# All elementwise work with two tensor inputs goes to the vector engine, and the tasks no longer name an engine

## The chip, the cores and the metric

The kernel runs on one core of one Trainium2 chip. The metric is the time of one execution on the device in microseconds, as the median of several runs. The core's engines are named as the profile names them: PE is TensorE (matrix products and transposes), PEld its weight loads, DVE is VectorE, ACT is ScalarE, POOL is GpSimd, SP is SyncE, which issues the loads.

## What is computed

A network of two layers over 256 latent tokens and 256 context tokens, model width 1024. Each layer has a half-step feed-forward part, a token mixer, and a second half-step feed-forward part. Each of these three is normed on the way in and on the way out, and its shift, scale and gate come from a conditioning vector:

```python
def half_ffn(x, mod, k, norm_g, w):
    h = modulated_norm(x, mod, k, norm_g)          # rms_norm * (1 + scale) + shift
    return gated_residual(x, swiglu(h, *w), mod, k, norm_g, FFN_RESIDUAL)   # x + weight*gate*rms_norm(y)
...
y, y_c = token_mixers(h, hc, not last, ...)        # windowed attention, dense attention, mLSTM; merged; @ w_out
x = gated_residual(x, y, mod, 1, norm_g[l], 1.0)
x = half_ffn(x, mod, 2, norm_g[l], ffn2)
if not last:
    ctx = gated_residual(ctx, y_c, mod_c, 1, norm_g[l], 1.0)
    ctx = half_ffn(ctx, mod_c, 2, norm_g[l], ffn2)
```

The hidden width of the feed-forward part is 2816. All data are float32, and the output is the latent stream, 256 x 1024.

## The kernel before

A float32 product is made of three products of two shorter parts. Each operand is split into a high part (a copy into the type fp32r, by ScalarE) and a low part (the value less its high part); `mm3` (L192) multiplies high by high, high by low and low by high (L194 to L196). Weights come in units of 128 partitions by up to 1024 columns, 512 KB. `cvt_unit` (L155) converts one: `hi` on ScalarE (L162), `lo` by a two-input subtraction (L163) on the engine that the task names. `run_tasks` (L167) walks through a list of tasks, each a triple of weight units, a function and a list of engines; it converts units two tasks ahead of their use and issues their loads on SP's queue three units further ahead. There are four buffers for raw units and five each for `hi` and `lo`; a raw buffer comes free when its `lo` is done, and the next load into it waits for that.

The parts in order of time, in microseconds of the profiled execution: feed-forward part of layer 0 (to about 400), its mixer (to 1000), its second feed-forward part (to 1345), the first of layer 1 (to 1738), its mixer (to 2110), and the last, for the latent tokens only.

The end of each part is a chain of norms. `closing` (L503) finishes the output half by half. `post_half` (L552) takes square sums on ScalarE (L560) and multiplies each half by its gate (L563); `post_finish` (L566) computes the inverse root of the mean square and updates the residual (L574); `prenorm_stat` (L437) takes the square sums of the new rows (L444), an inverse root again, and writes the normalised rows `t` (L449 on VectorE, L451 on ScalarE), which TensorE transposes (L466) for the next part. The inverse root is `rsqrt` (L205): a seed and three Newton steps on columns of 1, 2, 8 or 16 numbers, each instruction waiting for the one before (L211 to L220). A part is done for the latent and then the context tokens, so each change of part has two such chains.

In the mixer, `q_rows` (L751) rotates the rows of the normed queries (`rope`, L743 to L749) or scales them (`times_g`, L774); `k_rows` (L790 on) norms and rotates the keys; `k_cols` (L813) splits their transposes (L826 to L828). `logsig` (L1104 to L1126) computes the forget gates of the mLSTM. The attention scores are written at L1012, and L1043 scales some of the probabilities on GpSimd, with one tensor input and a column of factors.

Tables name the engines: `BOTH_E`, `ONE_E`, `EARLY_E` and `GP` put some of the feed-forward units' subtractions on GpSimd, and the wrapper `pool(...)` in `mixer_tasks` those of most of the query, value and convolution units. The rest go to VectorE. The order of the instructions on each engine is not written out: a scheduler chooses it when the kernel is built, from the tasks' order, a priority (`urgent`) and its own estimates of durations. Each engine then runs its list in order.

## Time and profile before

| | |
|---|---|
| median of 3 runs | 2339.59 us (2339.14 to 2345.08) |
| span of the profiled execution, its own time | 2339.1 us |
| TensorE busy | 2243.5 us, 96% |
| VectorE busy | 1574.0 us, 67%, 2709 instructions |
| ScalarE busy | 1025.0 us, 44% |
| GpSimd busy | 198.7 us, 8%, 115 instructions |
| chain that ended last | TensorE 83%, VectorE 11%, ScalarE 4%, GpSimd 0% |
| mean granted clock of TensorE | 0.98 |

The chain is followed back from the last instruction, at each step to what released it. The granted clock is a share of TensorE's full speed; the two levels that occur are 1 (2.4 GHz) and 0.5 (1.2 GHz). A wait is put down to the engine whose work came last.

### The profile page before, as it was taken

The page shows a single profiled execution, that of the slowest core. Times are in us where ns is not written, and L with a number is a line of the kernel's source. Part 1 is how long each engine was busy: PE and PEld are TensorE (multiplying, and loading weights), DVE is VectorE, ACT ScalarE, POOL GpSimd, SP SyncE. Part 2 cuts the span into 40 slices and gives each one's busy share as a digit, 9 for nine tenths or more (in the row PEclk, how much of TensorE's full clock was granted, in tenths as well). Part 3 has the DMA queues.
Part 4 walks back from the last instruction along what each step waited for, and adds up shares of the span by engine and source line. Part 5 has one row for each costly group of instructions (what it writes and reads, how often), then busy time and mean ns, then how long its engine had stood idle before and what let it go on. Part 6 is the DMA issues. An engine that isn't in the chain of part 4 may idle for free.

```text
span 2339.1 us, 30561 instructions
## 1 busy us (share of the span) xinstructions
PE 2243.5 (96%) x11666; PEld 1848.6 (79%) x11666; DVE 1574.0 (67%) x2709; ACT 1025.0 (44%) x1637; POOL 198.7 (8%) x115
## 2 busy tenths in 40 slices
PE   7999999899999999999999989999999899996998
PEld 4877777776678888888878788787878668996997
DVE  3987775788776654664444378778768677867555
ACT  3322222567887433442222253222235488754443
POOL 0000001123410000200000020000012220003001
PEclk9999999999999999999999999999999899998999
DMA  7756563411122224434343327656643103464664
GB/s 274 224 191 184 164 215 103 133 63 38 37 89 75 81 84 135 138 122 135 117 126 117 113 90 221 193 186 192 194 126 118 55 28 118 154 227 143 189 186 144
DMA packets 123523, 322.98 MB, mean 138 GB/s; under 512 B 12392, under 2 KB 25768, under 8 KB 122608
## 3 DMA queue, kind: packets, MB, share of 16 engines
q1 hardware_dynamic: 110224, 309.83, 41.8%
q10 hardware_dynamic: 13152, 11.21, 1.6%
q8 instruction: 91, 1.49, 0.3%
q14 instruction: 56, 0.46, 0.1%
HBM read 316.72 MB, written 4.28 MB: 137 GB/s over the span
## 4 chain that ended last, share of the span: by engine, by line
PE 83%; DVE 11%; ACT 4%; issue 1%; DMA 1%; POOL 0%; ACTq 0%; DVEq 0%
PE ps L194 25%; PE ps L195 25%; PE ps L196 25%; PE ps L1244 1%; PE ps L1015 1%; DVE sm L220 1%; PE ps L1055 1%; DVE lo L163 1%; PE ps L1012 1%; DVE sm L219 1%; PE ps L364 1%; PE ps L1213 1%; DVE slot L574 1%; PE ps L1070 1%; PE ps L466 1%
## 5 line engine op out<-in xcount | busy, mean ns | idle before, releaser
L162 ACT ACTIVATE hi<-raw 128x1024 fp32r<-128x1024 f32 (+1 forms) x444 | 456.0, 1031 | 769.7 <-PE ps L195 261.8
L194 PE MATMUL ps<-slot,hi 128*128 128x512 f32 (+1 forms) x2232 | 777.6, 350 | 7.1 <-ACT slot L189 4.9
L195 PE MATMUL ps<-slot,hi 128*128 128x512 f32 (+1 forms) x2232 | 775.8, 348 | 0.5 <-DVE slot L190 0.4
L196 PE MATMUL ps<-slot,lo 128*128 128x512 f32 (+1 forms) x2232 | 773.3, 347 | 0.0
L163 DVE TENSOR_TENSOR lo<-raw,hi 128x1024 fp32r<-128x1024 f32 (+2 forms) x395 | 475.1, 1205 | 287.6 <-ACT hi L162 285.6
L194 PEld LDWEIGHTS ps<-slot,hi 128*128 128x128 f32 x2232 | 419.6, 189 | 75.6 <-ACT slot L189 7.1
L196 PEld LDWEIGHTS ps<-slot,lo 128*128 128x128 f32 x2232 | 421.1, 189 | 57.5
L195 PEld LDWEIGHTS ps<-slot,hi 128*128 128x128 f32 x2232 | 421.0, 189 | 56.1 <-DVE slot L190 1.4
L194 PE MATMUL ps<-hi,slot 128*128 128x512 f32 (+2 forms) x1048 | 404.4, 386 | 3.0 <-DVE slot L828 1.9
L195 PE MATMUL ps<-lo,slot 128*128 128x512 f32 (+2 forms) x1048 | 402.0, 384 | 4.0 <-DVE lo L163 2.5
L196 PE MATMUL ps<-hi,slot 128*128 128x512 f32 (+2 forms) x1048 | 401.4, 384 | 2.9 <-DVE slot L190 2.9
L356 DVE SCALAR_TENSOR_TENSOR t<-raw,sc,t 128x1024 f32<-128x1024 f32 x224 | 280.4, 1281 | 130.8 <-DMA raw<-in_w_ada_dram 130.6
L194 PEld LDWEIGHTS ps<-hi,slot 128*128 128x128 f32 x1048 | 199.0, 190 | 49.1 <-issue 8.9
L196 PEld LDWEIGHTS ps<-hi,slot 128*128 128x128 f32 x1048 | 198.8, 190 | 44.3 <-DVE slot L190 3.1
L195 PEld LDWEIGHTS ps<-lo,slot 128*128 128x128 f32 x1048 | 199.0, 190 | 43.8 <-DVE lo L163 4.9
L163 POOL TENSOR_TENSOR lo<-raw,hi 128x1024 fp32r<-128x1024 f32 (+1 forms) x49 | 116.8, 2389 | 683.4 <-ACT hi L162 508.8
L189 ACT ACTIVATE slot<-t 128x512 fp32r<-128x512 f32 (+1 forms) x138 | 80.3, 594 | 183.4 <-DVE t L606 158.1
L563 POOL TENSOR_TENSOR slot<-slot,slot 128x512 f32<-128x512 f32 x20 | 30.3, 1524 | 1321.4 <-DMA raw<-in_w_down_dram 733.3
L606 DVE TENSOR_TENSOR t<-ps,t 128x512 f32<-128x512 f32 (+1 forms) x88 | 54.7, 622 | 87.9 <-PE ps L196 86.7
L190 DVE TENSOR_TENSOR slot<-t,slot 128x512 fp32r<-128x512 f32 (+1 forms) x138 | 88.6, 651 | 6.9 <-ACT slot L189 6.5
L1017 DVE TENSOR_REDUCE sm<-ps 128x1 f32<-128x512 f32 (+1 forms) x96 | 55.9, 593 | 13.1 <-PE ps L1015 12.6
L466 PE MATMUL ps<-ident,t 128*128 128x128 f32 x176 | 30.5, 331 | 34.4 <-DVE t L449 33.4
(194 smaller groups left out, 1911.3 us busy)
## 6 DMA issues: line engine op xcount, KB each, us to landing
raw<-in_w_gu_dram SPq DMA_DIRECT2D x176, 512.0 KB
raw<-in_w_ada_dram SPq DMA_DIRECT2D x128, 512.0 KB
raw<-in_w_down_dram SPq DMA_DIRECT2D x92, 512.0 KB
raw<-in_w_fm_dram SPq DMA_DIRECT2D x64, 512.0 KB
raw<-in_w_br_dram SPq DMA_DIRECT2D x24, 512.0 KB
raw<-in_w_out_dram SPq DMA_DIRECT2D x24, 512.0 KB
slot<-in_w_ada_dram SPq DMA_DIRECT2D x16, 512.0 KB
raw<-in_w_down_dram SPq DMA_DIRECT2D x20, 256.0 KB
```

Of the source, the lines that this page charges most:

```text
L162: self.nc.scalar.activation(out=hi, in_=raw, func=AF.Copy)
L163: eng.tensor_tensor(out=lo, in0=raw, in1=hi.bitcast(F32), op=ALU.subtract)
L189: self.nc.scalar.activation(out=hi, in_=src, func=AF.Copy)
L190: self.nc.vector.tensor_tensor(out=lo, in0=src, in1=hi.bitcast(F32), op=ALU.subtract)
L194: mm(out, lh, rh, start=start, stop=False, **kw)
L195: mm(out, lh, rl, start=False, stop=False, **kw)
L196: mm(out, ll, rh, start=False, stop=stop, **kw)
L356: v.scalar_tensor_tensor(out=acc, in0=units[0], scalar=c, in1=acc, op0=ALU.mult, op1=ALU.add)
L466: nc.tensor.transpose(pt[:, o:o + P], xn[b][:, c * P:(c + 1) * P], self.ident)
L563: eng.tensor_tensor(out=self.y_half(st, tb, n), in0=src[q], in1=self.Gt[tb // 2][:, n * 512:(n + 1) * 512], op=ALU.mult)
L606: nc.vector.tensor_tensor(out=hid[:, :W], in0=ps[:, :W], in1=hid[:, :W], op=ALU.mult)
L1017: v.tensor_reduce(out=mx[:, :1], in_=ps[:, :nkey], axis=AX.X, op=ALU.max)
```

## The change

Every weight subtraction is issued on VectorE, and so are all the products with the gate (L563), the rotation and the scaling of the query rows. The tables of engines and the wrapper are gone, and a task's optional third entry is now the look-ahead. L1043 stays on GpSimd. Comments are removed, so lines move up by four to ten.

```diff
-    def cvt_unit(self, st, eng):
+    def cvt_unit(self, st):
...
-        eng.tensor_tensor(out=lo, in0=raw, in1=hi.bitcast(F32), op=ALU.subtract)
+        self.nc.vector.tensor_tensor(out=lo, in0=raw, in1=hi.bitcast(F32), op=ALU.subtract)
...
-            want = min(len(keys), use + (rest[1] if len(rest) > 1 else LA_CVT))
+            want = min(len(keys), use + (rest[0] if rest else LA_CVT))
...
-        out = [one(ga, i) for i in range(nu)] + [(keys[1], both, BOTH_E(v, g))]
+        out = [one(ga, i) for i in range(nu)] + [(keys[1], both)]
...
-        return out + [(*one(gb, i), [ONE_E(v, g)[i]], *la(i)) for i in range(nu)]
+        return out + [(*one(gb, i), *la(i)) for i in range(nu)]
...
-            eng = nc.vector if ds or (last and q == 0) else nc.gpsimd
-            eng.tensor_tensor(out=self.y_half(st, tb, n), in0=src[q], in1=self.Gt[tb // 2][:, n * 512:(n + 1) * 512],
-                              op=ALU.mult)
+            nc.vector.tensor_tensor(out=self.y_half(st, tb, n), in0=src[q], in1=self.Gt[tb // 2][:, n * 512:(n + 1) * 512],
+                                    op=ALU.mult)
...
-                eng = nc.gpsimd if part == 0 and q < GP else nc.vector
-                out.append(([("gu", l, i, f0 + q // 2, q % 2)], gu(q // 2, q % 2), [eng]))
+                out.append(([("gu", l, i, f0 + q // 2, q % 2)], gu(q // 2, q % 2)))
...
-            self.rope(u, q, 8, tb, self.cosg[0], self.sing[0], nc.gpsimd, q)
+            self.rope(u, q, 8, tb, self.cosg[0], self.sing[0], q)
         else:
-            self.times_g(q, q, 8, 0, nc.gpsimd)
+            self.times_g(q, q, 8, 0)
...
-        side = gates[:1] + pool(qb[:1]) + gates[1:2] + pool(qb[1:] + vm_[nv:va]) + gates[2:] + pool(vm_[va:vb]) + qcols(1) + pool(vm_[vb:])
+        side = gates[:1] + qb[:1] + gates[1:2] + qb[1:] + vm_[nv:va] + gates[2:] + vm_[va:vb] + qcols(1) + vm_[vb:]
         na = 4 * len(qtb)
-        out += weave(att[:na], side) + weave(att[na:], pool(conv))
+        out += weave(att[:na], side) + weave(att[na:], conv)
```

The scheduler's order shifts with it. Three places show how.

VectorE between the second layer's mixer and the last feed-forward part, in the second half of the first tokens' norm chain. Before (`sm` are the inverse root's columns, L563 the gate product, `lo` a weight's low part):

```order
L574 SCALAR_TENSOR_TENSOR slot_17592<-slot_17646,sm_17703,slot_17592 128x1024
L163 TENSOR_TENSOR lo_17760<-raw_17666,hi_17759 128x1024
L211 TENSOR_SCALAR sm_17717<-sm_17714 128x1
L212 TENSOR_SCALAR sm_17718<-sm_17717 128x1
L216 SCALAR_TENSOR_TENSOR sm_17719<-sm_17718,sm_17717 128x1
L220 SCALAR_TENSOR_TENSOR sm_17718<-sm_17719,sm_17718 128x1
L563 TENSOR_TENSOR slot_17646<-ps_17730,slot_17590 128x512
L216 SCALAR_TENSOR_TENSOR sm_17719<-sm_17718,sm_17717 128x1
```

After the change VectorE has, from the same residual update on:

```order
L567 SCALAR_TENSOR_TENSOR slot_17592<-slot_17646,sm_17703,slot_17592 128x1024
L159 TENSOR_TENSOR lo_17773<-raw_17668,hi_17772 128x1024
L159 TENSOR_TENSOR lo_17791<-raw_17670,hi_17790 128x1024
L206 TENSOR_SCALAR sm_17717<-sm_17714 128x1
L556 TENSOR_TENSOR slot_17646<-ps_17730,slot_17590 128x512
L207 TENSOR_SCALAR sm_17718<-sm_17717 128x1
L159 TENSOR_TENSOR lo_17880<-raw_17763,hi_17879 128x1024
L211 SCALAR_TENSOR_TENSOR sm_17719<-sm_17718,sm_17717 128x1
L159 TENSOR_TENSOR lo_17884<-raw_17776,hi_17883 128x1024
L215 SCALAR_TENSOR_TENSOR sm_17718<-sm_17719,sm_17718 128x1
L556 TENSOR_TENSOR slot_17646<-ps_17765,slot_17590 128x512
```

Subtractions that stood in GpSimd's list now stand between the steps of the inverse root.

VectorE at the split of the keys in the second layer's mixer. Before, `s` are the forget gates' numbers, the copy and subtraction at L827 and L828 split the keys:

```order
L1115 TENSOR_TENSOR s_2530_14631<-s_2529_14630 128x32
L1116 TENSOR_SCALAR s_2531_14632<-s_2530_14631 128x32
L1118 SCALAR_TENSOR_TENSOR s_2531_14632<-s_2531_14632,s_2530_14631 128x32 x7
L1119 SCALAR_TENSOR_TENSOR s_2531_14632<-s_2531_14632,s_2529_14630 128x32
L1120 TENSOR_SCALAR s_2531_14632<-s_2531_14632 128x32
L1121 SCALAR_TENSOR_TENSOR s_2531_14632<-s_2527_14627,s_2531_14632 128x32
L1126 COPY s_2532_14650<-s_2531_14632 128x4x4 x2
L827 COPY slot_14529<-slot_14529 64x512
L828 TENSOR_TENSOR slot_14529<-ps_14530,slot_14529 64x512
```

After the change, from the gate add (L1097) at the same place on, VectorE has:

```order
L1097 TENSOR_TENSOR s_2527_14627<-gm_14463,gateb_13948 128x64
L1100 SCALAR_TENSOR_TENSOR s_2528_14629<-s_2527_14627 128x32
L1115 COPY s_2532_14650<-s_2527_14627 128x4x4 x2
L159 TENSOR_TENSOR lo_15131<-raw_14499,hi_15130 128x1024
L818 COPY slot_14529<-slot_14529 64x512
L819 TENSOR_TENSOR slot_14529<-ps_14530,slot_14529 64x512
L818 COPY slot_14541<-slot_14541 64x512
L819 TENSOR_TENSOR slot_14541<-ps_14542,slot_14541 64x512
L778 TENSOR_TENSOR slot_14553<-ps_14555,slot_14553 64x4x128
```

The split stood behind the whole computation of the forget gates; now it stands ahead of it, behind one more weight subtraction.

TensorE between the first feed-forward part and the mixer of layer 0; `ps_3074` and `ps_3081` are outputs of the feed-forward part, `ps_3116` on receives the transposes of the normalised rows. Before:

```order
L194 MATMUL ps_3081<-hi_2912,slot_2252 128x512
L195 MATMUL ps_3081<-lo_2913,slot_2252 128x512
L196 MATMUL ps_3081<-hi_2912,slot_2254 128x512
L466 MATMUL ps_3116<-ident,t_480_3011 128x128
L466 MATMUL ps_3116<-ident,t_481_3013 128x128
```

After the change, at the same place, TensorE has, once the products with `hi_2912` are done:

```order
L190 MATMUL ps_3074<-lo_3069,slot_2253 128x512
L191 MATMUL ps_3074<-hi_3068,slot_2255 128x512
L461 MATMUL ps_3116<-ident,t_480_3011 128x128
L461 MATMUL ps_3126<-ident,t_480_3011 128x128
L461 MATMUL ps_3136<-ident,t_480_3011 128x128
```

The product with the unit `hi_3068`, `lo_3069` stood behind the transposes; now six of its matrix products stand ahead of them, of which the first two rows are the last.

## Rows read from the trace of the kernel before

**Rows 1.** The page, part 1: busy us, share of the span, instructions, by engine.

```profile
PE 2243.5 (96%) x11666; PEld 1848.6 (79%) x11666; DVE 1574.0 (67%) x2709; ACT 1025.0 (44%) x1637; POOL 198.7 (8%) x115
```

**Rows 2.** Windows: length, busy of PE, PEld, DVE, ACT, POOL, then PEclk, DMA, GB/s.

```profile
400.00:446.00 46.00, 39.42 (x183) 32.09 (x182) 38.83 (x78) 24.48 (x44) 9.75 (x6) 0.96 0.38 121
465.00:496.00 31.00, 26.00 (x165) 23.02 (x164) 26.28 (x60) 15.95 (x28) 9.86 (x5) 0.94 0.27 85
1336.00:1396.00 60.00, 53.82 (x311) 46.80 (x311) 41.98 (x78) 28.38 (x53) 20.29 (x11) 0.94 0.26 83
1726.00:1800.00 74.00, 66.27 (x316) 55.60 (x315) 59.45 (x113) 37.49 (x63) 21.88 (x16) 0.93 0.42 131
1800.00:1851.00 51.00, 42.59 (x215) 32.93 (x215) 36.16 (x90) 20.51 (x39) 14.37 (x6) 0.80 0.23 73
2098.00:2142.00 44.00, 26.09 (x115) 21.01 (x114) 36.68 (x56) 20.02 (x32) 17.98 (x7) 0.81 0.53 165
2310.00:2339.00 29.00, 17.59 (x73) 13.44 (x72) 18.21 (x32) 8.28 (x14) 6.82 (x4) 0.83 0.30 100
```

**Rows 3.** Timeline, TensorE from 420: start, length, instruction, idle time before.

```profile
420.57 3.64 PE L466 MATMUL ps<-ident,t 128*128 128x128 f32 x15 [4.52 <-DVE t L449]
```

**Rows 4.** Waits of TensorE: total us, times, longest us.

```profile
PE ps L466 <- DVE t L449: 33.4, 8, 10.1
```

**Rows 5.** Timelines of VectorE and GpSimd from 404.

```profile
404.60 0.16 DVE L219 TENSOR_TENSOR sm<-sm,sm 128x2 f32<-128x2 f32 x1
404.80 2.34 DVE L220 SCALAR_TENSOR_TENSOR sm<-sm,sm 128x2 f32<-128x2 f32 x1
404.73 2.40 POOL L163 TENSOR_TENSOR lo<-raw,hi 128x1024 fp32r<-128x1024 f32 x1 [1.17 <-ACT hi L162]
```

**Rows 6.** The chain that ended last, in five places: start, us, what.

```profile
402.42 1.17 DVE sm L211
...
476.82 2.31 DVE sm L219
...
1348.18 2.39 DVE sm L220
...
1738.02 2.40 DVE sm L220
...
2322.26 1.23 DVE sm L220
```

**Rows 7.** Timelines of GpSimd and VectorE from 1934.

```profile
1934.35 1.57 POOL L1043 TENSOR_SCALAR t<-t,sm 128x512 f32<-128x512 f32 x1 [2.01 <-issue]
1935.40 1.23 DVE L163 TENSOR_TENSOR lo<-raw,hi 128x1024 fp32r<-128x1024 f32 x1
```

**Rows 8.** Groups by line, GpSimd: busy us, mean ns, idle time before.

```profile
L163 POOL TENSOR_TENSOR lo<-raw,hi 128x1024 fp32r<-128x1024 f32 (+1 forms) x49 | 116.8, 2389 | 683.4 <-ACT hi L162 508.8 <-DVE sm L216 163.5 <-DVE sm L220 3.6
L1043 POOL TENSOR_SCALAR t<-t,sm 128x512 f32<-128x512 f32 (+1 forms) x24 | 32.5, 1354 | 92.4 <-DVE sm L1037 88.0 <-PE ps L1055 2.4 <-issue 2.0
L563 POOL TENSOR_TENSOR slot<-slot,slot 128x512 f32<-128x512 f32 x20 | 30.3, 1524 | 1321.4 <-DMA raw<-in_w_down_dram 733.3 <-ACT t L560 586.2 <-issue 1.9
```

**Rows 9.** The page, part 5: the weight subtraction on VectorE.

```profile
L163 DVE TENSOR_TENSOR lo<-raw,hi 128x1024 fp32r<-128x1024 f32 (+2 forms) x395 | 475.1, 1205 | 287.6 <-ACT hi L162 285.6
```

**Rows 10.** The chain that ended last, from 1830.

```profile
1830.26 0.42 DVE slot L827
...
1835.73 0.77 PE ps L1012
```

**Rows 11.** The chain that ended last, from 2109.

```profile
2109.45 2.27 DVE sm L216
...
2128.74 0.75 DVE t L449
```

**Rows 12.** Window in the first attention, columns as in rows 2.

```profile
500.00:700.00 200.00, 192.33 (x980) 144.43 (x979) 156.61 (x394) 154.51 (x322) 54.25 (x36) 0.99 0.16 50
```

**Rows 13.** Timeline of ScalarE from 2120.

```profile
2120.41 1.06 ACT L162 ACTIVATE hi<-raw 128x1024 fp32r<-128x1024 f32 x1 [3.54 <-DMA raw<-in_w_gu_dram]
```

More of the change, by code (lines that the diff above doesn't have):

```diff
@@ L57 @@
 AX_ = 3
-GP = 5
 QB = 4
-BOTH_E = lambda v, g: [v, v, v, v]
-ONE_E = lambda v, g: [v, g, v, g]
-EARLY_E = lambda v, g: [g, v, g, v, g]
 LA_CVT = 2
@@ L168, in run_tasks @@
         keys = [k for t in tasks for k in t[0]]
-        engs = [e for t in tasks for e in (t[2] if len(t) > 2 and t[2] else [self.nc.vector] * len(t[0]))]
         raws, ready = {}, {}
@@ L178, in run_tasks @@
                     nd += 1
-                ready[ncv] = self.cvt_unit(raws.pop(ncv), engs[ncv])
+                ready[ncv] = self.cvt_unit(raws.pop(ncv))
                 ncv += 1
@@ L332, in mk @@
             return fn
-        return [([("ada0", h, k)], mk(k), [v], 0 if h else LA_CVT) for k in range(0, NK, 2)]
+        return [([("ada0", h, k)], mk(k), 0 if h else LA_CVT) for k in range(0, NK, 2)]
     def ada_tasks(self, l, ms):
@@ L543, in closing @@
         nu = len(keys[0])
-        v, g = self.nc.vector, self.nc.gpsimd
-        out = [one(ga, i) for i in range(nu)] + [(keys[1], both, BOTH_E(v, g))]
+        out = [one(ga, i) for i in range(nu)] + [(keys[1], both)]
         la = lambda i: [max(LA_END, min(LA_CVT, nu - 1 - i))] if len(streams) == 1 else []
-        return out + [(*one(gb, i), [ONE_E(v, g)[i]], *la(i)) for i in range(nu)]
+        return out + [(*one(gb, i), *la(i)) for i in range(nu)]
     def urgent(self, yes=True):
@@ L648, in ffn_tasks @@
                 keys = [("gu", l, i, q // 2, q % 2) for q in range(first)]
-                engs = EARLY_E(nc.vector, nc.gpsimd)[:first]
                 if halves:
@@ L652, in ffn_tasks @@
                     out.insert(AT, ([], rest))
-                    out += weave([([], early_half(0, 1, n), None, 0) for n in range(first)], halves)
-                    out += [([], early_half(1, s, n), None, 0) for s in range(2) for n in range(first)]
+                    out += weave([([], early_half(0, 1, n), 0) for n in range(first)], halves)
+                    out += [([], early_half(1, s, n), 0) for s in range(2) for n in range(first)]
                 else:
-                    out.append((keys, early, engs))
+                    out.append((keys, early))
             for q in range(first, 2 * nf):
-                eng = nc.gpsimd if part == 0 and q < GP else nc.vector
-                out.append(([("gu", l, i, f0 + q // 2, q % 2)], gu(q // 2, q % 2), [eng]))
+                out.append(([("gu", l, i, f0 + q // 2, q % 2)], gu(q // 2, q % 2)))
             if final:
@@ L735, in by_stream, with rope @@
         return [([k for ks, _ in tasks for k in ks], fn)]
-    def rope(self, dst, src, nh, tb, cos, sin, eng=None, out=None):
-        v = eng or self.nc.vector
+    def rope(self, dst, src, nh, tb, cos, sin, out=None):
+        v = self.nc.vector
         t = self.t512()[:, :nh * 64]
@@ L766, in q_rows, with times_g @@
             u = self.t512()
-            self.rope(u, q, 8, tb, self.cosg[0], self.sing[0], nc.gpsimd, q)
+            self.rope(u, q, 8, tb, self.cosg[0], self.sing[0], q)
         else:
-            self.times_g(q, q, 8, 0, nc.gpsimd)
-    def times_g(self, dst, src, nh, w, eng=None):
+            self.times_g(q, q, 8, 0)
+    def times_g(self, dst, src, nh, w):
         g = self.gqk[:, w, :].unsqueeze(1).to_broadcast([P, nh, 64])
         h3 = lambda x: x.rearrange("p (h d) -> p h d", d=64)
-        (eng or self.nc.vector).tensor_tensor(out=h3(dst), in0=h3(src), in1=g, op=ALU.mult)
+        self.nc.vector.tensor_tensor(out=h3(dst), in0=h3(src), in1=g, op=ALU.mult)
     def q_cols(self, Q, q, tb):
@@ L905, in mixer_tasks @@
         conv = [self.conv_task(l, c, ms, R, need_ctx) for c in range(8)]
-        pool = lambda ts: [(ks, fn, [nc.gpsimd] * len(ks)) for ks, fn, *_ in ts]
         mrg = [self.merge_tasks(l, n, ms, R, qs) for n in range(3)]
```

## Prediction

> **What bounds the kernel now.** I read the shares of busy time first, then the idle time of TensorE by the engine that ends it, then windows around the places where it falls, and only then the instructions that move. TensorE is busy for 2243.5 of 2339.1 us, VectorE for 1574.0, GpSimd for 198.7 [rows 1]. On average, then, neither the engine that loses work nor the one that gains it is the bound, and the change can pay or cost only where TensorE stands idle behind VectorE. These places are short. Seven windows hold most of them: length minus TensorE's busy time gives 6.6, 5.0, 6.2, 7.7, 8.4, 17.9 and 11.4 us, 63 us together [rows 2]. In the same windows the mean granted clock is below 1. At its lower level (1.2 instead of 2.4 GHz) a matmul takes twice as long; length times one minus the mean clock is 1.8, 1.9, 3.6, 5.2, 10.2, 8.4 and 4.9 us, 36 us [rows 2], part of it inside the idle time. Around 420 the low level follows an idle time of 4.52 us of TensorE, and the first 15 transposes after it take 3.64 us [rows 3]. What ends the idle time is most often the normalised row of VectorE (L449): 33.4 us in 8 waits [rows 4].
>
> **What GpSimd does to VectorE.** At 404.60 a 128x2 instruction of the rsqrt takes 0.16 us; the next takes 2.34 us and ends as the GpSimd subtraction that began at 404.73 ends (2.40 us) [rows 5]. From every VectorE instruction that overlaps GpSimd I subtracted the usual length of its form: 57 of them lose over 0.25 us each, 84 us together. The first is L211 at 402.42, 1.17 us long, the last L220 at 2322.26, 1.23 us [rows 6]. None of the 57 reads PSUM. Nearly all of the loss lies against GpSimd's two-input instructions. Against its one-input scaling, L1043, there is next to none: a VectorE subtraction that began while an L1043 ran took its usual 1.23 us [rows 7].
>
> The Trainium skill (SBUF — State Buffer, "Who interferes with whom") calls this an exclusive lock on a port pair that the two engines share, and lets a VectorE instruction with two SBUF inputs contend with any GpSimd instruction that reads SBUF. The trace agrees for two-input instructions of GpSimd and differs for L1043. By the page the 24 L1043 that stay on GpSimd, 32.5 us, would go on blocking, and more of the moved subtractions would run into them; by the row nothing is charged, and the row decides.
>
> **Part by part: the move.** What moves are 49 weight subtractions (116.8 us on GpSimd), 20 gate products (30.3 us) and, as 115 less 49, 20, 24 and 4 memsets, 18 instructions of the query rows, 198.7 - 116.8 - 30.3 - 32.5 = 19 us [rows 1, 8]. On VectorE a subtraction takes 1.21 us [rows 9], so 49 cost 57 us, four of them being half as large; a product has half the elements, at 0.6 to 0.7 us 13 us; the 18 others, at the same ratio of about one half, 9 to 10. VectorE gains some 80 us of work and loses 84 us of blocking: its total stays. What changes is place and length. A weight's low part is ready in 1.2 instead of 2.4 us, and its raw buffer, which the next load waits for, comes free sooner. And 57 waits leave chains in which only those moved instructions come back that stand ahead in VectorE's order.
>
> **Part by part: the places.** For each: blocked time in the chain, less the moved work that now stands in it, then what TensorE makes of that.
>
> First FFN to mixer (400 to 446). Five pieces of the chain are blocked ahead of the row at L449, the first 1.17 us [rows 6], the longest 2.34 [rows 5], 6.3 us above their usual lengths. Three products of 0.65 and two subtractions (1.2 and half of it) come in, 3.8 us, partly while VectorE waits for ScalarE anyway, so the row comes 2.5 to 3 us earlier. In TensorE's new order six products stand ahead of the transposes: the idle 4.52 us is filled, the clock need not fall, and the second chain starts sooner. Bounds: 2.8, the row alone, and 6.5; nearest to the whole gap with its clock, 4.52 + 1.8, I take 6.
>
> Key norm (465 to 496). Four blocked pieces like the one at 476.82 [rows 6], 6 to 7 us, less three subtractions, 3.6: 3 to 5, I take 4, with some of the clock.
>
> Second FFN to the next layer's first (1336 to 1396). The first place again: five pieces like that at 1348.18 [rows 6], 7.4 us, less 4.5 moved in; 3.7 to 7.7, I take 7.
>
> That FFN to the mixer (1726 to 1800). The same, five pieces like that at 1738.02 [rows 6], 6.3 us; behind it the rotation of the queries, which blocks VectorE for 2 to 3 us and now costs it about 4.4 of its own while TensorE's waits there end earlier. 4 to 10, I take 7.
>
> Keys of the second mixer (1800 to 1851). VectorE runs the whole log-sigmoid chain first and begins the split of the keys at 1830.26; the first score matmul starts at 1835.73 [rows 10]. In the new order two subtractions and then the splits stand ahead of the log-sigmoid. From the gate add at 1821.6 that is 2 x 1.2 us and some 4 us of splits: the scores could start near 1828.5. The log-sigmoid's own 6 us are paid later beside attention. 4 to 10, I take 6.
>
> Mixer to last FFN (2098 to 2142). Seven pieces are blocked, from 2109.45 on, 14.3 us, ahead of the row at 2128.74 [rows 11]. Seven subtractions come in, 8.5 us: 5.8 left if their weights are there. TensorE has nothing else to do, so the idle time shrinks and stays. 4 to 6.5, I take 5.
>
> The end (2310 to 2339). Two blocked pieces, the last at 2322.26 [rows 6], 3.2 us; three subtractions and a product come in, before and beside them: 0 to 3, I take 2.
>
> Attention of the first mixer (500 to 700). TensorE is busy for 192 of 200 us, VectorE for 157 [rows 12]; some 19 us of moved work come for 15 us of blocking: 0, with 3 us either way. The second mixer's attention and the stretches between likewise: 0, with 3 us either way.
>
> Sum: 6 + 4 + 7 + 7 + 6 + 5 + 2 = 37 us. The low ends with both attentions at -3: 2.8 + 3 + 3.7 + 4 + 4 + 4 + 0 - 6 = 15.5. The high ends: 6.5 + 5 + 7.7 + 10 + 10 + 6.5 + 3 + 6 = 55. The profiled execution took its span, 2339.1 us, half a microsecond under the median of 2339.59. Forecast: 2339 - 37 = 2302, between 2284 and 2324.
>
> **The rivals.** Half the gain: the next thing is late. Behind the freed row stand ScalarE's copies and weights that have not landed (ScalarE's conversion at 2120.41 has waited 3.54 us for a load [rows 13]). Then the idle time shrinks by the earlier row alone and the low clock stays: 7 to 15 us, 2324 to 2332.
>
> No change: 80 us of work takes the place of 84 us of blocking in the same engine, and the chains end when they did, 2333 to 2346. For it: the two totals. Against it: the seven windows, where the moved work is shorter than the blocking. [...]
>
> Slower: VectorE works in order, and a subtraction whose weights are late now holds the rsqrt chain behind it, which it did not do from GpSimd's queue. The price is VectorE's idle time ahead of a subtraction, 287.6 us over 395, 0.73 each [rows 9]. For 49 that is 36 us: 2357 with half of it on the path, 2375 with all. It decides from the point where a high part comes later than VectorE reaches its subtraction; the place is the mixer to the last FFN, where loads are late [rows 13]. Against it: most of that idle time is VectorE with nothing else to do.
>
> **How the numbers follow.** Forecast (2284 to 2324) 0.70, half the gain 0.12, no change 0.10, slower 0.08. A measurement tells about 0.3%, 7 us, from no change, so faster means below 2332.6: 0.82, the same 0.10, slower 0.08. The range leaves out the slower case, nearly all of no change and a little below the forecast: 2284 to 2335.
>
> **What would show it.** In the changed kernel's profile GpSimd has 28 instructions and some 33 us; the small pieces of the rsqrt take 0.15 to 0.25 us everywhere; VectorE's busy time stays within 20 us of 1574; TensorE's waits for L449 fall from 33.4 to about 15 us; the mean clock rises in the windows from 400, 1336 and 1726; the first score of the second mixer comes 6 us sooner after its rows than before. The prediction would be wrong if VectorE stood idle inside the rsqrt chains for a high part, if TensorE's idle time stayed, or if new idle time grew in the attentions.

## The result, and the profile after

The changed kernel takes 2285.3 us in the median of five runs (2281.5 to 2295.7) against 2339.6: the ratio is 0.977, with a 95% interval of 0.976 to 0.979. The gain is 54 us where 37 were forecast, and the time lies inside the stated range, near its lower end. The profiled execution is the longest of the five, with a span of 2293.9 us; it is compared below with the one of before, so 45 us are to be found there. Executions of the changed kernel go with the mean granted clock: 0.985 in this one, 0.990 to 0.994 in the other four.

The page's part 1 and the engine shares of its chain (part 4), as in [rows 1]:

```profile
PE 2234.2 (97%) x11666; PEld 1844.0 (80%) x11666; DVE 1551.5 (68%) x2796; ACT 1025.0 (45%) x1637; POOL 32.7 (1%) x28
...
PE 91%; DVE 4%; ACT 2%; DMA 1%; issue 1%; ACTq 0%; POOL 0%; DVEq 0%
```

GpSimd keeps the 24 scalings. In the chain VectorE's share falls from 11% to 4%. VectorE does 87 instructions more and is busy for 22 us less, 1551.5 after 1574.0.

The windows that answer to [rows 2] and, last, to the attention of [rows 12] (length; busy time of PE, PEld, DVE, ACT, POOL; PEclk; DMA; GB/s). They cover the same work, the last one from what was 496 on; the first three are 6, 5 and 8 us shorter:

```profile
400.00:440.00 40.00, 37.32 (x182) 30.32 (x181) 34.86 (x84) 24.45 (x44) 0.00 (x0) 1.00 0.43 140
459.00:485.00 26.00, 25.21 (x173) 22.82 (x173) 22.36 (x59) 14.53 (x28) 0.00 (x0) 1.00 0.24 81
1331.00:1383.00 52.00, 50.96 (x310) 44.25 (x308) 39.05 (x89) 28.49 (x53) 0.00 (x0) 1.00 0.31 96
1714.00:1779.00 65.00, 63.74 (x334) 53.65 (x333) 56.29 (x129) 37.74 (x65) 0.00 (x0) 1.00 0.47 150
1779.00:1817.00 38.00, 37.57 (x217) 30.71 (x215) 31.63 (x96) 20.46 (x39) 0.00 (x0) 1.00 0.30 97
2064.50:2101.00 36.50, 25.41 (x113) 20.80 (x112) 29.22 (x63) 20.13 (x31) 0.00 (x0) 0.81 0.61 198
2268.00:2293.90 25.90, 16.88 (x74) 13.39 (x72) 17.69 (x36) 8.28 (x15) 0.00 (x0) 0.89 0.33 112
485.00:697.00 212.00, 203.39 (x991) 152.55 (x989) 162.64 (x429) 156.62 (x326) 19.94 (x16) 0.94 0.16 51
```

In the first five TensorE's idle time, length less busy, goes from 6.6, 5.0, 6.2, 7.7 and 8.4 us to 2.7, 0.8, 1.0, 1.3 and 0.4, and the clock from 0.96, 0.94, 0.94, 0.93 and 0.80 to 1.00. In the sixth 11 us stay of 17.9 and the clock with them, in the seventh 9.0 of 11.4. The last, the attention, is where time is given back: its clock is 0.94.

TensorE's waits for the normalised row, as in [rows 4], and the two groups that answer to [rows 8, 9], by line:

```profile
PE ps L461 <- DVE t L444: 14.3, 5, 6.2
```

```profile
L159 DVE TENSOR_TENSOR lo<-raw,hi 128x1024 fp32r<-128x1024 f32 (+1 forms) x444 | 526.7, 1189 | 283.2 <-ACT hi L158 281.2
...
L1033 POOL TENSOR_SCALAR t<-t,sm 128x512 f32<-128x512 f32 (+1 forms) x24 | 32.5, 1354 | 1879.2 <-DVE sm L1027 1262.7 <-DMA sinkr<-in_sink_dram 594.9 <-issue 12.6
```

The first place on VectorE's timeline, which answers to [rows 5]:

```profile
404.82 0.16 DVE L213 TENSOR_TENSOR sm<-sm 128x2 f32<-128x2 f32 x1
405.02 0.16 DVE L214 TENSOR_TENSOR sm<-sm,sm 128x2 f32<-128x2 f32 x1
405.10 1.23 DVE L159 TENSOR_TENSOR lo<-raw,hi 128x1024 fp32r<-128x1024 f32 x1
406.24 0.15 DVE L215 SCALAR_TENSOR_TENSOR sm<-sm,sm 128x2 f32<-128x2 f32 x1
```

The steps of the rsqrt here now take 0.15 to 0.16 us. The subtraction at 405.10 starts inside the step at 405.02, and the next step starts as the subtraction ends, 1.22 us after the last one instead of 0.20: of its 1.23 us the subtraction costs the chain 1.0, since the records of the step and the subtraction lie over each other.

To see where the gain lies, the starts of the instructions of VectorE and ScalarE that have the same tiles in both traces were subtracted from each other at the ends of each stretch (times of before; the median of the nine nearest; us gained, a minus is time given back). The two middle columns are two executions of the changed kernel, the last is the run "one input" below, in which nothing moves:

| stretch of before | forecast | changed, first | changed, second | one input |
|---|---|---|---|---|
| 400 to 446, first FFN to mixer | 6 | 6.1 | 6.0 | 2.7 |
| 465 to 496, key norm | 4 | 6.0 | 6.0 | 5.3 |
| 496 to 700, attention | 0 | -8.4 | -2.1 | 4.6 |
| 700 to 1010 | 0 | 1.5 | 1.5 | 1.6 |
| 1336 to 1396, FFN to FFN | 7 | 7.9 | 7.9 | 5.9 |
| 1726 to 1800, FFN to mixer | 7 | 9.2 | 9.3 | 3.3 |
| 1800 to 1851, keys of the second mixer | 6 | 12.7 | 12.7 | 7.0 |
| 1851 to 2095 | 0 | -0.2 | -2.7 | -0.1 |
| 2095 to 2142, mixer to last FFN | 5 | 7.2 | 7.5 | 7.9 |
| 2142 to the end | 2 | 4.4 | 4.3 | 2.6 |

The key split of the second mixer, which answers to [rows 10]: the gate add and the first score before, and then, after the change, the gate add, the one subtraction behind it, the split and the first score:

```profile
1821.58 0.23 DVE L1107 TENSOR_TENSOR s<-gm,gateb 128x64 f32<-128x64 f32 x1
1835.73 0.77 PE L1012 MATMUL ps<-slot,slot 128*128 128x512 f32 x1 [8.41 <-DVE slot L787]
```

```profile
1797.47 0.22 DVE L1097 TENSOR_TENSOR s<-gm,gateb 128x64 f32<-128x64 f32 x1
...
1798.88 1.23 DVE L159 TENSOR_TENSOR lo<-raw,hi 128x1024 fp32r<-128x1024 f32 x1 [0.79 <-ACT hi L158]
1800.13 0.42 DVE L818 CAST slot<-slot 64x512 fp32r<-64x512 f32 x1
1805.06 0.47 PE L1002 MATMUL ps<-slot,slot 128*128 128x512 f32 x1 [0.43 <-DVE slot L819]
```

The chain of the last FFN, which answers to [rows 11]: the first sum before, and then the chain after the change:

```profile
2107.99 0.15 DVE L570 TENSOR_TENSOR sm<-pss 128x1 f32<-128x1 f32 x1
```

```profile
2074.29 0.15 DVE L563 TENSOR_TENSOR sm<-pss 128x1 f32<-128x1 f32 x1
...
2079.46 2.35 DVE L159 TENSOR_TENSOR lo<-raw,hi 128x1024 fp32r<-128x1024 f32 x2
...
2082.45 1.22 DVE L159 TENSOR_TENSOR lo<-raw,hi 128x1024 fp32r<-128x1024 f32 x1
...
2083.84 1.22 DVE L159 TENSOR_TENSOR lo<-raw,hi 128x1024 fp32r<-128x1024 f32 x1
...
2086.41 1.22 DVE L159 TENSOR_TENSOR lo<-raw,hi 128x1024 fp32r<-128x1024 f32 x1 [0.48 <-ACT hi L158]
...
2089.34 0.75 DVE L444 TENSOR_SCALAR t<-slot,sm 128x1024 f32<-128x1024 f32 x1
```

The first score stands 0.43 us behind TensorE's last product instead of 8.4. In the last FFN's chain the row at L444 comes 15.1 us after the first sum at 2074.29; before it was 20.8 us (from 2107.99 to 2128.74 [rows 11]). Only one subtraction there, at 2086.41, made VectorE wait for its high part, for 0.48 us.

### The profile page after: what moved, and what is told of

Read it like the earlier page. It is cut to its first block, busy times and chain, and to the rows that moved or that the text cites. A ratio compares the mean times of both kernels' runs of the same rounds, so it can differ in the third digit from the quotient of the medians.

```text
span 2293.9 us, 30523 instructions
## 1 busy us (share of the span) xinstructions
PE 2234.2 (97%) x11666; PEld 1844.0 (80%) x11666; DVE 1551.5 (68%) x2796; ACT 1025.0 (45%) x1637; POOL 32.7 (1%) x28
## 3 DMA queue, kind: packets, MB, share of 16 engines
q8 instruction: 91, 1.49, 0.3%
## 4 chain that ended last, share of the span: by engine, by line
PE 91%; DVE 4%; ACT 2%; DMA 1%; issue 1%; ACTq 0%; POOL 0%; DVEq 0%
PE ps L189 27%; PE ps L190 27%; PE ps L191 27%; PE ps L1045 2%; PE ps L1005 1%; PE ps L1234 1%; PE ps L1002 1%; PE ps L1060 1%; PE ps L1062 1%; PE ps L359 1%; PE ps L1203 1%; PE ps L461 1%; DMA sinkr<-in_sink_dram 1%; DVE lo L159 0%; DMA slot<-in_x_dram 0%
## 5 line engine op out<-in xcount | busy, mean ns | idle before, releaser
L159 DVE TENSOR_TENSOR lo<-raw,hi 128x1024 fp32r<-128x1024 f32 (+1 forms) x444 | 526.7, 1189 | 283.2 <-ACT hi L158 281.2
L185 DVE TENSOR_TENSOR t<-ps,t 128x512 fp32r<-128x512 f32 x80 | 54.4, 685 | 10.0 <-ACT t L184 9.4
L184 ACT ACTIVATE t<-ps 128x512 fp32r<-128x512 f32 x80 | 46.0, 595 | 32.7 <-PE ps L1045 32.4
L1033 POOL TENSOR_SCALAR t<-t,sm 128x512 f32<-128x512 f32 (+1 forms) x24 | 32.5, 1354 | 1879.2 <-DVE sm L1027 1262.7
```

The source lines that it names most:

```text
L159: self.nc.vector.tensor_tensor(out=lo, in0=raw, in1=hi.bitcast(F32), op=ALU.subtract)
L184: self.nc.scalar.activation(out=hi, in_=src, func=AF.Copy)
L185: self.nc.vector.tensor_tensor(out=lo, in0=src, in1=hi.bitcast(F32), op=ALU.subtract)
L1033: nc.gpsimd.tensor_scalar(out=t[:, :nkey], in0=t[:, :nkey], scalar1=r[:, e:e + 1], scalar2=None, op0=ALU.mult)
```

## Experiments

**The changed kernel again.** No edit. 

> The changed kernel once more, for a second profiled execution of it. In the first (span 2293.9 us) the mean granted clock was 0.985; in four others it was 0.990 to 0.994 and the spans 2279.7 to 2286.0. Theory: the difference of about 10 us between executions is time at the lower clock in the first mixer's attention (0.83 and 0.65 in the windows 510 to 530 and 530 to 550 of the first), not more waiting. Expected: span 2280 to 2287, the clock near 1.0 in those two windows, TensorE's total idle time between instructions within 3 us of the first's 50.7. Rival: the idle time itself differs from run to run; then the clock there stays low and the idle time differs by 5 us or more.

Measured: 2284.7 us (2283.3 to 2290.0), ratio 0.977 (0.976 to 0.978); the profiled execution spans 2288.2 us. TensorE's idle time, all gaps between its instructions summed, is 49.9 us against 50.7, and before it was 86.6. The span is 1 us above the expected bounds. The windows of the attention, of the first execution and then of this one:

```profile
510.00:530.00 20.00, 17.75 (x92) 12.69 (x90) 16.32 (x48) 11.50 (x25) 0.00 (x0) 0.83 0.06 14
530.00:550.00 20.00, 17.61 (x63) 13.43 (x63) 14.47 (x42) 10.91 (x25) 0.00 (x0) 0.65 0.04 17
```

```profile
510.00:530.00 20.00, 17.23 (x89) 11.58 (x86) 16.59 (x49) 11.70 (x25) 0.00 (x0) 0.91 0.09 27
530.00:550.00 20.00, 17.78 (x90) 14.29 (x90) 17.18 (x52) 13.36 (x32) 0.00 (x0) 0.91 0.01 4
```

The waits agree within a microsecond and the clock does not. What differs between executions of this kernel is time at the low clock: 0.83 and 0.65 against 0.91 and 0.91 in these two windows, some 7 us, which is the difference of the attentions in the table. The clock did not come to 1.0 as expected: TensorE's waits of 2.3 and 1.0 us just ahead of these stretches are in both executions.

**Only the weights move.**

```diff
 # before
-        eng.tensor_tensor(out=lo, in0=raw, in1=hi.bitcast(F32), op=ALU.subtract)
+        self.nc.vector.tensor_tensor(out=lo, in0=raw, in1=hi.bitcast(F32), op=ALU.subtract)
```

> Of the change only one part: the 49 weight subtractions go to VectorE; the gate products and the query rows' rotation and scaling stay on GpSimd. Theory (blocking): 67.9 of the 84 us that VectorE lost to GpSimd lay against these subtractions, so four fifths of the gain of 54 us come from this part: 2290 to 2305, and VectorE still loses 10 to 16 us to GpSimd. Rival (length of the product chains: gate products and rotation matter more than the subtractions, since they sit in the norm chains themselves): 2315 to 2330.

Measured: 2295.2 us, ratio 0.981 (0.979 to 0.983). VectorE still loses 19 us to GpSimd, in 20 instructions, 3 more than expected at most. The gain is 44 us, four fifths of the whole, as the blocking had it.

**Only the rest moves.**

```diff
 # before
-            eng = nc.vector if ds or (last and q == 0) else nc.gpsimd
+            eng = nc.vector
...
-            self.rope(u, q, 8, tb, self.cosg[0], self.sing[0], nc.gpsimd, q)
+            self.rope(u, q, 8, tb, self.cosg[0], self.sing[0], nc.vector, q)
-            self.times_g(q, q, 8, 0, nc.gpsimd)
+            self.times_g(q, q, 8, 0, nc.vector)
```

> The other part of the change alone: gate products, rotation and scaling go to VectorE, the 49 weight subtractions stay on GpSimd. Theory (blocking): VectorE still loses some 65 to 75 us to the subtractions: 2325 to 2340. Rival (the products matter more): 2295 to 2315. If the two parts add up, this gain and that of the weights alone make about 54 us.

Measured: 2327.4 us, ratio 0.995 (0.994 to 0.997). VectorE loses 70 us. TensorE's waits in this run:

```profile
PE ps L466 <- DVE t L449: 28.3, 9, 9.5
...
PE ps L1012 <- DVE slot L787: 8.9, 2, 8.7
```

Of the 33.4 us [rows 4] only 5 are gone, and the wait for the second mixer's keys is untouched. The two parts add up: 44.4 + 12.2 = 56.6 us against 55 for both.

**One input, nothing moved.**

```diff
 # before
-        eng.tensor_tensor(out=lo, in0=raw, in1=hi.bitcast(F32), op=ALU.subtract)
+        if eng is self.nc.gpsimd:
+            eng.tensor_scalar(out=lo, in0=raw, scalar1=2.0 ** -13, scalar2=None, op0=ALU.mult)
+        else:
+            eng.tensor_tensor(out=lo, in0=raw, in1=hi.bitcast(F32), op=ALU.subtract)
```

> The kernel before with one edit: where GpSimd subtracts the high part from a weight it instead scales the raw weight by 2^-13, one tensor input in place of two, so the computation of those 49 low parts is left out. The order of instructions on TensorE, VectorE, ScalarE and SyncE is the one of before. Theory (VectorE is blocked by two-input instructions of GpSimd, and not by one-input ones as the scalings in attention show): VectorE's losses fall from 84 us to 11 to 20 (those against gate products and rotation), though GpSimd is as busy as before (a 128x1024 in 2.4 to 3.0 us), and the time falls by 20 to 40 us, to 2300 to 2320, with no work moved at all. Rival (the gain of the change comes from shorter subtractions, earlier buffers and the new order, blocking is a symptom): 2335 to 2345. Second rival (any GpSimd instruction that reads SBUF blocks): losses stay near 84 us, 2335 to 2345.

Measured: 2297.1 us, ratio 0.982 (0.981 to 0.984): 42.5 us faster with the order of before and GpSimd busy for longer than before, 217.7 us. That is 3 us more than the theory's bounds allowed, although VectorE's losses fell less than it said, from 84 to 30 us, half of them against the scalings, in 21 instructions. The first place shows them (timelines of VectorE and GpSimd, then GpSimd's group by line):

```profile
404.68 0.88 DVE L221 TENSOR_TENSOR sm<-sm 128x2 f32<-128x2 f32 x1
405.60 0.16 DVE L222 TENSOR_TENSOR sm<-sm,sm 128x2 f32<-128x2 f32 x1
405.79 0.16 DVE L223 SCALAR_TENSOR_TENSOR sm<-sm,sm 128x2 f32<-128x2 f32 x1
404.50 2.78 POOL L164 TENSOR_SCALAR lo<-raw 128x1024 fp32r<-128x1024 f32 x1
```

```profile
L164 POOL TENSOR_SCALAR lo<-raw 128x1024 fp32r<-128x1024 f32 (+1 forms) x49 | 135.5, 2765 | 624.9 <-PE ps L198 584.5 <-issue 35.2 <-ACT t L447 2.5
```

The scaling runs from 404.50 to 407.28. The VectorE step that begins at 404.68 is held until 405.56, 1.06 us after the scaling's start, and the steps behind it run at full speed beside the rest of it. So a one-input instruction of GpSimd holds VectorE too, but only for its first part; that the prediction saw almost none of it against L1043 was that few steps met that part. The blocking is the cause of most of the gain: the time falls without shorter work on GpSimd (2.77 us each in place of 2.39) and without a new order. One thing besides the blocking did change. The scaling does not read the high part, so it starts sooner, and the low part is done 1.5 us after ScalarE's conversion of the unit in the median instead of 2.5, which frees the raw buffer sooner too. No run separates this. TensorE's waits that end with a weight's low or high part are 2.5 and 0.8 us in all in the kernel before, by its list of waits, so little of the 42.5 us can come from it directly.

**The products too.**

```diff
 # the run on one input
+            if eng is nc.gpsimd:
+                eng.tensor_scalar(out=self.y_half(st, tb, n), in0=src[q], scalar1=0.5, scalar2=None, op0=ALU.mult)
+                continue
             eng.tensor_tensor(out=self.y_half(st, tb, n), in0=src[q], in1=self.Gt[tb // 2][:, n * 512:(n + 1) * 512],
                               op=ALU.mult)
```

> The kernel before with GpSimd's weight subtractions replaced by one-input scalings as in the run on one input (2297.1 us, VectorE's losses 31 us, 15 of them against the scalings and 16 against the two-input instructions that were left), and now its 20 gate products too (a scaling by 0.5 in place of the product with the gate, so the gates of those 20 halves are left out). The order on every other engine is the one of before, and no work moves. Theory (the gain of the change is the end of blocking, and the work that it moves costs next to nothing): VectorE's losses fall to 17 to 24 us and the time to 2284 to 2293, as low as the changed kernel's 2284.7. Rival (moving the products has a value of its own, since VectorE does one in 0.69 and GpSimd in 1.3 to 1.5 us): the time stays above 2293.

Measured: 2289.7 us, ratio 0.978 (0.976 to 0.979), inside the theory's bounds. VectorE's losses are 25 us, one more than expected at most. The half-size scaling holds VectorE for its first part as well:

```profile
401.81 0.48 DVE L214 TENSOR_SCALAR sm<-sm 128x2 f32<-128x2 f32 x1
402.33 0.17 DVE L215 TENSOR_SCALAR sm<-sm 128x2 int32<-128x2 int32 x1
401.66 1.49 POOL L567 TENSOR_SCALAR slot<-slot 128x512 f32<-128x512 f32 x1 [6.10 <-ACT t L563]
```

It starts at 401.66 and lasts 1.49 us; the step of VectorE ends at 402.29, 0.63 us in. The kernel that moves nothing but blocks for 25 us instead of 84 comes within 5 us of the changed one: freed chains are the gain. That the totals are so close is in part a cancellation. In the stretches of the table from 1726 and 1800 this run gains about 5 and 8 us where the changed kernel gains 9.2 and 12.7, and in the first mixer's attention it gains 5 to 6 us where the changed kernel gives back 2.1 to 8.4.

**The gates behind the keys.**

```diff
 # before, second layer only (R["need_ctx"] is set in mixer_tasks)
+            if not R["need_ctx"]:
+                K = R["K"][1]
+                one = R["gm"][64:, 0, 0:1]
+                v.scalar_tensor_tensor(out=one, in0=K[64:, 2, 0:1].bitcast(F32), scalar=0.0, in1=one, op0=ALU.mult, op1=ALU.add)
             g = self.small3([P, 4, 16], "gat")
```

> The kernel before with one edit in the second layer's mixer: the forget gates' computation first reads one number of the split keys (times 0, added to a gate number, so that nothing changes in value; one VectorE instruction more). So the key split stands ahead of the gates on VectorE, as in the changed kernel, while all subtractions stay where they were on GpSimd. In the changed kernel the window that was 1800 to 1851 gained 12.7 us, in the kernel before with unblocked weights 7.0, against 6 predicted. Theory (the order: the key split stood behind 8 us of gates, and the low clock followed the wait): 5 to 12 us less in that window, 2328 to 2335 in all, the wait of 8.4 us down to 2 to 4, since two subtractions on GpSimd still block the split for up to 4.9 us. Rival (only the blocking counts there): within 2 us of before, 2337 to 2342.

Measured: 2336.1 us, ratio 0.998 (0.997 to 1.000): 4.7 us in the median, 1 us short of the theory's bounds and 1 us beyond the rival's. In the profiled execution 6.5 us are gained from 1800 to the attention at 1900 to 2000, inside the theory's bounds for the window; at 1851 itself, where instructions have changed places, the gain reads as 5 to 8 us, depending on which are taken. TensorE, GpSimd and VectorE there:

```profile
1832.19 0.77 PE L1013 MATMUL ps<-slot,slot 128*128 128x512 f32 x1 [4.09 <-DVE slot L787]
1823.08 4.94 POOL L163 TENSOR_TENSOR lo<-raw,hi 128x1024 fp32r<-128x1024 f32 x2 [6.44 <-ACT hi L162]
1824.45 1.31 DVE L827 CAST slot<-slot 64x512 fp32r<-64x512 f32 x1 [2.21 <-ACT slot L826]
...
1826.51 1.80 DVE L827 CAST slot<-slot 64x512 fp32r<-64x512 f32 x1
```

The wait goes from 8.41 to 4.09 us by the order alone, although two subtractions on GpSimd still stretch copies of 0.42 us to 1.31 and 1.80. The order alone gives 6.5 us and the unblocked kernel in the old order 7.0; the 12.7 us of the changed kernel are both together.

**The scalings too.** The changed kernel with L1033 (L1043 before) on VectorE:

```diff
 # after
-                    nc.gpsimd.tensor_scalar(out=t[:, :nkey], in0=t[:, :nkey], scalar1=r[:, e:e + 1], scalar2=None,
+                    v.tensor_scalar(out=t[:, :nkey], in0=t[:, :nkey], scalar1=r[:, e:e + 1], scalar2=None,
```

> The changed kernel with the 24 probability scalings of the attentions moved from GpSimd to VectorE as well, so that GpSimd has no work. In the unblocked run a one-input instruction of GpSimd held VectorE for about the first 1.05 us of its 2.77 us, so the 24 scalings of 0.93 to 1.57 us may hold it a little too. Theory (they cost almost nothing where they are, and VectorE is 80% busy there): 2281 to 2289, within 4 us of the changed kernel's 2284.7. Rival (their 1.57 us sit in the chain of softmax, transposes and products, and VectorE does one in 0.4 us): 2272 to 2280.

Measured: 2287.9 us, ratio 0.978 (0.976 to 0.979): no difference from the changed kernel. The 24 scalings neither cost on GpSimd nor pay on VectorE.

**The row sums later.**

```diff
 # after
-        side = gates[:1] + qb[:1] + gates[1:2] + qb[1:] + vm_[nv:va] + gates[2:] + vm_[va:vb] + qcols(1) + vm_[vb:]
+        side = gates[:1] + qb[:1] + qb[1:] + gates[1:2] + vm_[nv:va] + gates[2:] + vm_[va:vb] + qcols(1) + vm_[vb:]
```

> The changed kernel with one step of the first mixer put later among the tasks: the row sums of the mLSTM gates come behind the second half of the queries' projections. In the changed kernel this step's 5.5 us of scans stand ahead of an attention split on VectorE, TensorE waits 2.26 us for it, and the attention from 496 to 700 gives back 2.1 to 8.4 us of what came before. Theory (this order is the cause): TensorE's wait there goes and 2 to 6 us are gained, 2278 to 2283. Rival (the attention loses because VectorE has more to do there, wherever the scans stand): within 3 us of 2284.7 or slower.

Measured: 2292.1 us, ratio 0.979 (0.977 to 0.981): not faster, if anything some microseconds slower. TensorE's longest wait in that half of the attention, in the changed kernel and then here:

```profile
521.93 0.39 PE L1060 MATMUL ps<-t,slot 128*128 128x256 f32 x1 [2.25 <-DVE t L185]
```

```profile
525.87 1.11 PE L1045 MATMUL ps<-ident,t 128*128 128x128 f32 x4 [3.03 <-ACT t L1017]
```

The wait for the split is gone and another, of 3.03 us behind ScalarE, has taken its place. The attention gave back 4.9 us. The position of the scans is not the cause.

**Subtractions held behind the chains.**

```diff
 # after: self.hold is a column of ones, computed from each normalised row of the last FFN's input
+        if self.hold is not None and key[:3] == ("gu", 1, 1) and key[3] < 2:
+            self.nc.vector.scalar_tensor_tensor(out=lo, in0=raw, scalar=self.hold, in1=hi.bitcast(F32), op0=ALU.mult, op1=ALU.subtract)
+        else:
+            self.nc.vector.tensor_tensor(out=lo, in0=raw, in1=hi.bitcast(F32), op=ALU.subtract)
...
                 nc.vector.tensor_scalar(out=xn, in0=xs[q], scalar1=r[:, q:q + 1], scalar2=None, op0=ALU.mult)
+                if st.get("last"):
+                    self.hold = self.cp.tile([P, 1], F32, name=f"hold{tb}")
+                    nc.vector.tensor_scalar(out=self.hold, in0=xn[:, 0:1], scalar1=0.0, scalar2=1.0, op0=ALU.mult, op1=ALU.add)
```

> The changed kernel with an order forced between the second layer's mixer and the last feed-forward part: four of the weight subtractions take a factor of 1 that is computed from the normalised rows, so that they cannot stand inside the two norm chains (their units are not needed before the chains are done; the result is the same, two small VectorE instructions more). Left of the wait there are 6.0 and 4.9 us in the changed kernel. Theory (the moved subtractions, 1.2 us each, are what is left in the chain, the price that the prediction put on them): the rows at the end of the chains come 4 to 6 us earlier, the waits fall to 5 to 7 us together, 2278 to 2281. Rival (weights that land late hold the subtractions, and so the products, anyway): the wait only moves behind the chains, 2283 to 2287.

Measured: 2286.6 us, ratio 0.977 (0.975 to 0.979): no difference. The chain on VectorE and TensorE's wait:

```profile
2068.29 0.15 DVE L570 TENSOR_TENSOR sm<-pss 128x1 f32<-128x1 f32 x1
...
2076.96 0.75 DVE L448 TENSOR_SCALAR t<-slot,sm 128x1024 f32<-128x1024 f32 x1
...
2085.12 0.15 DVE L210 TENSOR_SCALAR sm<-sm 128x1 f32<-128x1 f32 x1 [2.13 <-ACT t L443]
...
2086.84 0.75 DVE L448 TENSOR_SCALAR t<-slot,sm 128x1024 f32<-128x1024 f32 x1
2087.65 2.82 PE L468 MATMUL ps<-ident,t 128*128 128x128 f32 x12 [9.22 <-DVE t L448]
```

The first row comes 8.7 us after the first sum instead of 15.1. Five subtractions left this chain, and with them a gate product and steps of the second chain; together they had cost 6.4 us in it, about the price of the five. But the two waits of 10.9 us have become one of 9.2: the second chain, with a square sum of ScalarE that VectorE waits 2.13 us for, has a length of its own and now ends last. The mechanism was right and what it is worth was not.

**Some subtractions given back.** The changed kernel, with the first layer's convolution units on GpSimd again:

```diff
 # after
+        eng = self.nc.gpsimd if key[0] == "fm" and key[1] == 0 and key[2] < 8 else self.nc.vector
-        self.nc.vector.tensor_tensor(out=lo, in0=raw, in1=hi.bitcast(F32), op=ALU.subtract)
+        eng.tensor_tensor(out=lo, in0=raw, in1=hi.bitcast(F32), op=ALU.subtract)
```

> The changed kernel with eight weight subtractions given back to GpSimd: those of the first layer's eight convolution units, which lie in the second half of its attention (about 560 to 690). The attention from 496 to 700 is the one place where the changed kernel gives back time (2.1 and 8.4 us in two executions), while with nothing moved and GpSimd unblocked it gained 5. Theory (moved work costs where VectorE is 80% busy; there the blocking costs less than the work, since subtractions on GpSimd meet few two-input instructions): 1 to 5 us less than the changed kernel, 2280 to 2284. Rival (blocking costs as much as the work it replaces): within 2 us, 2283 to 2287, or slower.

Measured: 2286.8 us, ratio 0.976 (0.975 to 0.978). And with three value units more (the condition takes in `key[0] == "tok" and key[2] == "vm" and key[3][0] >= 2`):

> The same with three more subtractions given back to GpSimd, those of the memory's value units in the first half of that attention (about 495 to 560), where TensorE waits 2.3, 1.0 and 1.2 us in the changed kernel and the low clock follows. Theory as before, and the waits of that half go with the order: 2 to 8 us less than the changed kernel, 2277 to 2283. Rival: within 2 us of it, 2283 to 2287, or slower, since three subtractions of 2.4 us block VectorE there again.

Measured: 2287.9 us, ratio 0.978 (0.977 to 0.979). Both are the changed kernel's time: the rivals. With eleven subtractions back, VectorE loses 13 us in eight instructions, one of them here:

```profile
522.84 2.33 DVE L1026 TENSOR_TENSOR sm<-sm,sm 128x2 f32<-128x2 f32 x1
521.56 3.60 POOL L160 TENSOR_TENSOR lo<-raw,hi 128x1024 fp32r<-128x1024 f32 x1 [12.76 <-ACT hi L158]
```

A step of 0.16 us takes 2.33. In the attention, blocking and moved work weigh the same as far as these runs can tell, since the attention differs by 6 us between two executions of one kernel; and no version tried is faster than the changed kernel.

## Why the prediction was right

**The bound and the cause** held. TensorE stays the bound, the gain is at the windows where it waited for VectorE, and all 57 blocked instructions are unblocked: after the change none loses 0.25 us. That the blocking, and not the length of the subtractions or the order, carries most of it was argued ahead of the result and is shown by the runs on one input: 42.5 and 50.7 us without moving anything. What those runs leave open is the small share of low parts that are ready sooner.

**The move** was priced at 80 us of work for 84 us of blocking, VectorE's total staying within 20 us. It fell by 22.5. By the lengths of the instructions the moved work is 74 us and the rest became 81 us shorter, which makes 7; the other 15 are records that lie over each other, as at 405.02, and count once in the busy time. The size was off, to the good side.

**The places.** Seven of them were put at 37 us and give 53.5 in the first execution (6.1, 6.0, 7.9, 9.2, 12.7, 7.2 and 4.4). Two were right within 1 us (400 and 1336), four 2 us too small. The term that was mis-sized is the keys of the second mixer, 12.7 instead of 6, above its upper bound of 10. Its mechanism was right: from the gate add to the first score it is 7.6 us (1797.47 to 1805.06, foreseen 1821.6 to 1828.5, 6.9), and before 14.2. That it is so close has some luck in it, for one subtraction stands there and not two, with a wait of 0.79 us for its high part. What the step left out is the clock. That window had lost 10.2 us to the low clock and 8.4 to the wait [rows 2]; with the wait gone the clock did not fall, and the step took 6 of the 7 us that its own working gives and nothing for the clock. The log-sigmoid that it put beside attention cost 0.2 to 2.7 us there (1851 to 2095) at most. The same holds for the sum: in the first five windows 27.7 us of idle time went and 41.9 us were gained, so some 14 us are clock; by the granted clock TensorE lost 18 us of its busy time to the low level in these windows before, and none after. I had read the 36 us of lost clock [rows 2] and carried only a small part of them into the places.

The errors went one way in the places and the other way in the attention. Five of the seven places lie above their own upper bounds (5, 7.7, 10, 6.5 and 3 us, at 465, 1336, 1800, 2095 and the end), and 54 us is just short of the 55 to which the high ends add up. Two of the five executions, 2281.5 and 2282.7 us, are below the range's 2284; that the median lies inside it, by 1 us, is partly luck.

**The attention** was put at 0, give or take 3. It gave back 8.4 and 2.1 us in two executions, and 5 came as a gain where nothing moved. Its waits are the same in both executions and only 1 us longer than before; the rest is the clock, which falls after waits of 2.3 and 1.0 us there.

**The rivals.** No change and slower were far off. The slower one's mechanism, a subtraction that holds the chain for a late weight, showed only in small pieces: 0.35 and 0.48 us inside the inverse roots (at 1753.40 and 2086.41) and 0.79 us ahead of the key split (1798.88), so the sign named for it did come, too small to count. VectorE's idle time ahead of subtractions is 283.2 us over 444 now, 287.6 over 395 before [rows 9]. The half gain's mechanism shows only in the last two windows, from 2064 and 2268, where 11 and 9 us of idle time and the low clock stay; for the first of them the prediction had said so. The other remarks on what would be seen held, but for VectorE's busy time: 28 instructions and 32.7 us on GpSimd, 14.3 us of waits for L444 (foreseen 15), the clock up in the three windows named.

**The page against the row.** (SBUF is the memory that the engines work on; PSUM, the `ps` tiles, takes TensorE's products.) The Trainium skill (SBUF — State Buffer, "Who interferes with whom") has a VectorE instruction with two inputs in SBUF contend with any GpSimd instruction that reads SBUF, and the later of the two blocked fully until the first is done. For two-input instructions of GpSimd the trace of before agrees: 45 such VectorE instructions began inside one (by at least 0.05 us, with over 0.4 us of it left), and none ended before it. For one-input ones the truth is between the page and my charge of nothing: they hold VectorE for 1.06 of 2.78 us at 1024 elements and 0.63 of 1.49 at 512, 15 us for 49 of them. The row that I let decide could not tell: the subtraction in [rows 7] began 1.05 us into a scaling of 1.57. The same trace has a step that met the start of one and took 0.56 us instead of its usual 0.15:

```profile
1930.77 1.57 POOL L1043 TENSOR_SCALAR t<-t,sm 128x512 f32<-128x512 f32 x1
1930.92 0.56 DVE L1024 TENSOR_TENSOR sm<-sm,qsc 128x1 f32<-128x1 f32 x1
```

For the 24 that stayed it made no difference that a run could tell.

**What stays open.** How much of the 54 us is clock in a given execution: the same program spans 2280 to 2294 us with the clock between 0.994 and 0.985, and nothing tried here fixes where it falls.

## What to carry to other kernels

Before work is put on GpSimd because it is idle, look at what VectorE does at the same time: a two-input instruction there can cost VectorE its own length (2.34 of 2.40 us at 404.80 [rows 5]), and a chain of short dependent steps pays it at every step. Price a wait of TensorE together with the low clock that follows it; here, in five windows, that was half as much again. A replacement of the instruction that keeps the order but not the suspected conflict, even one that computes something else, separates the conflict from most of what moving work changes as well; look at what it changes itself, here the moment at which it can start.

## What the runs showed of the hardware

A one-input scaling on GpSimd holds VectorE's instructions with two inputs in SBUF (and the one-input TENSOR_SCALAR at 401.81 above) for its first 1.06 us of 2.78 (128x1024) or 0.63 of 1.49 (128x512) and then lets them run; a two-input subtraction of 2.40 us holds them to its end. VectorE instructions that read PSUM are not held: in the kernel before, 29 of them began inside a two-input instruction of GpSimd and took their usual lengths, as from 1928.67, 1929.53 and 1929.93, with 0.48, 0.48 and 0.68 us beside a subtraction that ran from 1928.42 to 1930.80.

A VectorE step of 0.16 us between two subtractions puts the second off by only 0.07 us: in the changed kernel seven such pairs start 1.20 to 1.22 us apart and twelve pairs with nothing between them 1.13 to 1.14, while in a chain of such steps each starts 0.20 us after the one before.
